# A decoder layer on one core: where the PSUM-freeing copies, the first left operand of the up projection and the block sums of the gates stand in the program

## The chip, the core and the metric

The kernel runs on one core of a Trainium2 chip. The metric is the device time of one execution in microseconds. The core has a matrix engine (PE, with its weight loads listed as PEld), a vector engine (DVE), a scalar engine (ACT), a general engine (POOL) and a sync engine (SP) that issues transfers. POOL issues transfers too, in this kernel most of the stores and the loads of large operands. Each engine works through its own list of instructions in the order in which the program gave them, and waits on semaphores where an instruction needs another engine's result.

## The reference

One pre-norm decoder layer on 1024 tokens plus 16 meta tokens, model width 1024, in float32. Cut to what matters here:

```
h = rms_norm(x, norm1_w)
(rq, rk, rv, rg, dq, dk, dv, cb, cc, cx, gates) = [h @ w_in[:, s:e] for s, e in column_bounds()]
ret  = retention(...) * silu(rg);  diff = diff_attention(...);  conv = cb * short_conv(cc * cx, conv_w)
g = sigmoid(gates).reshape(b, l, 3, 1024)
merged = g[:, :, 0] * (ret @ w_branch[0]) + g[:, :, 1] * (diff @ w_branch[1]) + g[:, :, 2] * (conv @ w_branch[2])
x = x + merged @ w_out
u = square(relu(rms_norm(x, norm2_w) @ w_up))       # 1024 -> 4096
y = rms_norm((x + u @ w_down)[meta tokens dropped], final_norm_w)
```

The inputs are float32 throughout, and so is the output of 1024 x 1024.

## The kernel before, in words

**Arithmetic.** Each float32 product is made of three matmuls on split operands (`split`, L134: ACT casts the high part, DVE subtracts it from the source for the low part): high times high, high times low, low times high. A matmul is 128 x 128 against 128 x 512.

**Stages.** First come the mixers and then the gates (24 column blocks, loop at L748), whose order a scheduler with a timeline of its own sets. The gates loop also builds, in `branch_sums` (L725), the right-hand operands of the branch projections and stores them to DRAM, and at the turn n = 14 loads the first four of them (`SET`, L764, issued by SP). From then on the order is written by hand, in the loop at L1218 under `tc.manual_schedule()`: what the loop calls first stands first in every engine's list. It walks over 170 steps: 42 for the three branch projections, 16 for the output projection, 56 for the up projection, 56 for the down projection. The branch, up and down projections use a scheme of seven products for a 2 x 2 block matrix product. The class `Quad` (L787) holds two such block products, the pairs p = 0 and 1. A step is one product i (0 to 6) of a quad for both pairs, that is two halves of 12 matmuls (6 in the last block of the down projection). The operands of the seven products are named B11, B21, T1, B22, T2, T3, T4 in this order; T1 to T4 are differences and sums of blocks.

**Banks.** PSUM has 8 banks. In a quad, one bank per pair (`ch`) accumulates the products 0, 4, 5, 6, and another (`pt`) product 1 and later 2 and 3. A product that goes on accumulating in a bank has to wait until what the bank held was read: product 3 waits for ACT's copy of product 2 (L849, `keep`), product 5 for ACT's copy after product 4 (also L849), product 6 for DVE's add after product 5. This add is the first line of `use`: L927 in the branches, L1122 in the up projection, and in the down projection L1174, which stands behind another add, L1173. In the opening of the up projection a new `pt` bank comes free only with the add after product 1 of the quad whose product 1 came before.

**Work beside the steps.** `prep` makes the left operands (weights) of the step two ahead: combinations of blocks on DVE (L816), then the cast on ACT and the subtraction on DVE (L135, L136). The ring `w` has 5 buffers for them, so a cast for step s + 2 needs the matmuls of an earlier half to be over. `evac` reads the finished banks. The table `work` holds further jobs by step, such as splits of right-hand operands (L136 with tile `op`) and `sums` (L1133), which builds the operands of the down projection out of the results of the up projection: four DVE operations, two casts, two subtractions for each pair. Their results lie in the ring `X` of 16 tiles and are stored to DRAM by POOL (L1108).

**The opening of the up projection** (from S0 + 10 on; E0 = step 58 is its first step). Its right-hand operands are the normalised results of the output projection: `normalise` (L1058), for T1 to T4 a difference (L1075, L1080), and the split into the tile `op`. Steps 58 to 63 do products 0 and 1 of the first three quads, and step 64 begins with product 2, which needs T1.

**Order in one turn s of the loop:** `evac` of step s-1 for pair 1; the left operands of step s+2, both pairs; the matmuls of pair 0, then of pair 1; the jobs of `work`; `evac` of step s for pair 0; loads.

```
            if 0 < s <= N:
                steps[s - 1][3](1)
            ...
            if 0 <= s + LP < N:
                steps[s + LP][1]()
            ...
            for fn in work.get(s, ()):
                fn()
            if 0 <= s < N:
                steps[s][3](0)
```

## Time and profile before

| what | value |
|---|---|
| time, median of 3 runs (lowest to highest) | 2417.67 us (2417.62 to 2418.17) |
| the profiled execution: its own time | 2421.53 us |
| the profiled execution: its span | 2419.7 us |
| mean granted TensorE clock over the span | 0.983 |
| PE busy | 2315.2 us, 96% |
| DVE busy | 1604.9 us, 66% |
| ACT busy | 1070.8 us, 44% |
| POOL busy | 483.4 us, 20% |

The rows quoted further down come from the profiled execution, whose span leaves out some 1.8 us of its own time; times of places in the program are counted from the span's start. The granted clock is 1.00 at 2.4 GHz and 0.50 at 1.2 GHz. Busy shares are means over stages with different limits, so the stages are read one by one.

### The profile page before, as it was taken

How to read it: one execution, taken by the hardware profiler on the slowest of the kernel's cores; microseconds unless marked ns; L12 is line 12 of the kernel's file. 1: busy time of each engine (PE TensorE's matmuls, PEld its weight loads, DVE VectorE, ACT ScalarE, POOL GpSimd, SP SyncE). 2: the span in 40 equal slices, each digit the busy share in tenths (PEclk: the TensorE clock that was granted, in tenths of full speed). 3: DMA queues.
4: the chain of work that ended last, by engine and by line, in shares of the span. 5: the costliest groups of instructions: out<-in, count | busy, mean ns of one | idle time of the engine just before them, and what ended most of it. 6: DMA issues, size and time to landing. Idle time of an engine off the chain costs nothing. (4 is left out here: it accounts for less than half of the span.)

```text
span 2419.7 us, 32940 instructions
## 1 busy us (share of the span) xinstructions
PE 2315.2 (96%) x11854; PEld 2001.1 (83%) x11854; DVE 1604.9 (66%) x3276; ACT 1070.8 (44%) x2079; POOL 483.4 (20%) x643
## 2 busy tenths in 40 slices
PE   7999999999999999999899999999688999999997
PEld 7999999999999999988688787778566777777776
DVE  6776776776765666576455458776656666777685
ACT  5554654644643333234233323344445555543344
POOL 2132233233122212213232010000003222100003
PEclk9999999999999999999999999999889999999998
DMA  3111111111111111119987385546135546655322
GB/s 137 36 52 46 44 52 45 45 53 44 40 58 36 53 53 44 53 57 370 410 322 281 129 329 217 201 133 203 61 104 195 179 161 252 253 195 199 123 87 70
DMA packets 124725, 328.13 MB, mean 136 GB/s; under 512 B 15376, under 2 KB 19600, under 8 KB 116496
## 3 DMA queue, kind: packets, MB, share of 16 engines
q1 hardware_dynamic: 84912, 159.27, 19.1%
q0 software_dynamic: 39648, 166.75, 17.8%
q8 instruction: 93, 1.52, 0.2%
q14 instruction: 72, 0.59, 0.1%
HBM read 219.52 MB, written 106.43 MB: 135 GB/s over the span
## 5 line engine op out<-in xcount | busy, mean ns | idle before, releaser
L161 PE MATMUL pmm<-H,whi 128*128 128x512 f32 (+3 forms) x1640 | 574.5, 352 | 17.6 <-ACT H L196 8.4
L162 PE MATMUL pmm<-H,whi 128*128 128x512 f32 (+3 forms) x1640 | 574.5, 351 | 2.0 <-DVE H L197 1.9
L163 PE MATMUL pmm<-H,wlo 128*128 128x512 f32 (+3 forms) x1640 | 573.1, 351 | 0.0
L840 PE MATMUL pb<-op,w 128*128 128x512 f32 x1176 | 472.7, 402 | 64.9 <-ACT t L849 24.9
L842 PE MATMUL pb<-op,w 128*128 128x512 f32 x1176 | 466.9, 397 | 0.0
L841 PE MATMUL pb<-op,w 128*128 128x512 f32 x1176 | 466.7, 397 | 0.0
L136 DVE TENSOR_TENSOR w<-raw,w 128x512 fp32r<-128x512 f32 (+1 forms) x400 | 263.8, 670 | 250.3 <-ACT w L135 246.8
L135 ACT CAST w<-raw 128x512 fp32r<-128x512 f32 (+1 forms) x400 | 237.2, 603 | 395.5 <-PE pb L842 195.1
L161 PEld LDWEIGHTS pmm<-H,whi 128*128 128x128 f32 x1640 | 309.5, 189 | 43.9 <-ACT H L196 8.4
L162 PEld LDWEIGHTS pmm<-H,whi 128*128 128x128 f32 x1640 | 310.3, 189 | 27.7 <-DVE H L197 2.8
L840 PEld LDWEIGHTS pb<-op,w 128*128 128x128 f32 x1176 | 224.5, 191 | 130.6 <-ACT t L849 32.3
L163 PEld LDWEIGHTS pmm<-H,wlo 128*128 128x128 f32 x1640 | 309.7, 189 | 24.4
L136 POOL TENSOR_TENSOR wlo<-raw,whi 128x512 fp32r<-128x512 f32 x142 | 192.8, 1359 | 594.0 <-ACT whi L135 539.6
L842 PEld LDWEIGHTS pb<-op,w 128*128 128x128 f32 x1176 | 224.3, 191 | 52.5 <-DVE w L136 0.9
L841 PEld LDWEIGHTS pb<-op,w 128*128 128x128 f32 x1176 | 224.8, 191 | 49.8 <-issue 0.2
L135 ACT CAST whi<-raw 128x512 fp32r<-128x512 f32 x192 | 118.6, 618 | 172.9 <-issue 82.6
L1108 POOL DMA_DIRECT2D d<-X x130 | 69.5, 540 | 284.4 <-ACT X L1124 163.5
L816 DVE TENSOR_TENSOR raw<-raw,raw 128x512 f32<-128x512 f32 (+1 forms) x176 | 111.5, 662 | 5.8 <-DMA raw<-w_branch 4.0
L378 ACT ACTIVATE B<-B,nb 128x144 f32<-128x144 f32 (+3 forms) x64 | 50.6, 791 | 99.4 <-DVE nb L377 99.1
L849 ACT COPY t<-pb 128x512 f32<-128x512 f32 x132 | 74.5, 581 | 39.1 <-PE pb L842 39.0
L754 ACT ACTIVATE t<-t 128x512 f32<-128x512 f32 x48 | 30.3, 632 | 132.1 <-DVE t L250 132.1
L880 POOL DMA_DIRECT2D op<-d x36 | 19.3, 540 | 289.9 <-PE pb L842 287.8
(290 smaller groups left out, 3817.2 us busy)
## 6 DMA issues: line engine op xcount, KB each, us to landing
op<-d POOLq DMA_DIRECT2D x55, 1024.0 KB, 8.5
raw<-w_in SPq DMA_DIRECT2D x192, 256.0 KB, 2.6
d<-X POOLq DMA_DIRECT2D x146, 256.0 KB, 4.1
d<-w POOLq DMA_DIRECT2D x60, 512.0 KB, 7.5
raw<-w_up SPq DMA_DIRECT2D x76, 256.0 KB, 4.4
raw<-w_down SPq DMA_DIRECT2D x56, 256.0 KB, 4.1
d<-t POOLq DMA_DIRECT2D x48, 256.0 KB, 5.2
raw<-d SPq DMA_DIRECT2D x48, 256.0 KB, 6.6
```

Of the source, the lines that this page charges most:

```text
L135: a.copy(out=hi, in_=src)
L136: (eng or v).tensor_tensor(out=lo, in0=src, in1=f32(hi), op=ALU.subtract)
L161: nc.tensor.matmul(pt, lhsT=hi[:, s], rhs=xh[:, c0:c0 + w], start=start, stop=False)
L162: nc.tensor.matmul(pt, lhsT=hi[:, s], rhs=xl[:, c0:c0 + w], start=False, stop=False)
L163: nc.tensor.matmul(pt, lhsT=lo[:, s], rhs=xh[:, c0:c0 + w], start=False, stop=stop)
L378: a.activation(out=pt, in_=pt, func=AF.Exp, scale=slope, bias=nb, accum_out=st[:, m:m + 1])
L816: comb = lambda d, x0, x1, o: v.tensor_tensor(out=d, in0=x0, in1=x1, op=o)
L840: nc.tensor.matmul(pt, lhsT=w[0][:, s], rhs=b[0][:, k], start=first, stop=False, skip_group_check=True)
L841: nc.tensor.matmul(pt, lhsT=w[0][:, s], rhs=b[1][:, k], start=False, stop=False, skip_group_check=True)
L842: nc.tensor.matmul(pt, lhsT=w[1][:, s], rhs=b[0][:, k], start=False, stop=k == nk - 1, skip_group_check=True)
L849: a.copy(out=t, in_=pt)
L1108: at(fetch, now[0] + 1, lambda: G.dma_start(out=dst, in_=src))
```

## The change

It has three parts.

1. The loop of the hand-ordered steps. A new entry `copy` of each step takes the readings that free a bank within the quad: ACT's copies after products 2 and 4, and the add after product 5. In turn s, the copy of step s-1 for pair 1 now comes first, then `evac` of step s-1 for both pairs; the left operands of step s+2 come behind the matmuls of step s, and the copy of step s for pair 0 stands between the cast of the first and that of the second left operand, ahead of the jobs of `work`. `evac` of pair 0 thus moves from the end of turn s to the start of turn s+1, and the job `sums` of pair 0, which is entered one turn after it, moves one turn later. In `down_use` the add that reads the bank comes before the add that does not. The results (0, 0) of the pairs 4 and 5 of the up projection stay in the tile `t` of their copy.
2. The opening of the up projection. The differences of all blocks come first and the splits behind them, not block by block in turn; and the operands T2, T3, T4 are spread over the turns E0+4 to E0+8, before E0+4 to E0+6.
3. The gates. The block sums take every second turn from n = 6 on, and the loads of `SET` are entered one operand at a time at n = 9, 11, 13, 15, before all at n = 14.

```
+    SET = {}
...
-        if n >= 2 and sums_todo and n != 14:
+        if n >= 2 and sums_todo and (n < 6 or n % 2 == 0):
             branch_sums(*sums_todo.pop(0))
-        if n == 14:
...
-            for name in ORDER[:4]:
-                SET[name] = [opnd(True, [P, 4, 512]) for _ in range(2)]
-                for z in range(2):
-                    nc.sync.dma_start(out=f32(SET[name][z]), in_=TD[2][name][:, z])
+        if 9 <= n < 17 and n % 2 == 1:
+
+            name = ORDER[(n - 9) // 2]
+            SET[name] = [opnd(True, [P, 4, 512]) for _ in range(2)]
+            for z in range(2):
+                nc.sync.dma_start(out=f32(SET[name][z]), in_=TD[2][name][:, z])
...
-        def prep(self, i):
+        def prep(self, i, half):
...
-            for p in range(2):
+            for p in range(2) if half == 0 else ():
...
-            for p in range(2):
-                self.op(i, p, r[p, (0, 1, 4, 1, 4, 0, 3)[i]])
+            self.op(i, half, r[half, (0, 1, 4, 1, 4, 0, 3)[i]])
...
+        def keep(self, pt):
+            t = temp("t", [P, 512])
+            a.copy(out=t, in_=pt)
+            return t
+
+        def copy(self, i, p):
+
+            if i == 5:
+                self.use(p, 1, 1, self.kept["ch", p], self.kept["p5", p])
+            elif i == 2:
+                self.kept["p5", p] = self.keep(self.kept["pt", p])
+            elif i == 4:
+                self.kept["u2", p] = self.keep(self.kept["ch", p])
...
-            elif i == 2:
-                K["p5", p] = keep(K["pt", p])
             elif i == 4:
-                self.use(p, 0, 1, K["pt", p], keep(K["ch", p]))
-            elif i == 5:
-                self.use(p, 1, 1, K["ch", p], K["p5", p])
+                self.use(p, 0, 1, K["pt", p], K["u2", p])
...
     def up_t1(ks):
         for k in ks:
             normalise(0, 1, k)
-            v.tensor_tensor(out=blk(0, 1, k), in0=blk(0, 1, k), in1=blk(0, 0, k), op=ALU.subtract)
-            up_op("T1", k, blk(0, 1, k))
-
-    def up_sum(name, dst, x0, x1):
-        for k in range(4):
-            v.tensor_tensor(out=blk(*dst, k), in0=blk(*x0, k), in1=blk(*x1, k), op=ALU.subtract)
-            up_op(name, k, blk(*dst, k))
+        differ((0, 1), (0, 1), (0, 0), ks)
+        up_ops("T1", (0, 1), ks)
...
-    at(work, E0 + 1, lambda: up_t1(range(2)))
-    at(work, E0 + 2, lambda: up_t1(range(2, 4)))
-    at(work, E0 + 3, lambda: plain_op("B22", range(4)))
-    at(work, E0 + 4, lambda: up_sum("T2", (1, 1), (1, 1), (0, 1)))
-    at(work, E0 + 5, lambda: up_sum("T3", (0, 0), (1, 1), (0, 0)))
-    at(work, E0 + 6, lambda: up_sum("T4", (1, 0), (1, 0), (1, 1)))
...
+    for n, fn in ((1, lambda: up_t1((0, 1))), (2, lambda: up_t1((2, 3))), (3, lambda: up_plain("B22", range(4))),
+                  (4, lambda: differ((1, 1), (1, 1), (0, 1))), (5, lambda: up_ops("T2", (1, 1), range(4))),
+                  (6, lambda: differ((0, 0), (1, 1), (0, 0))), (6, lambda: up_ops("T3", (0, 0), range(4))),
+                  (7, lambda: differ((1, 0), (1, 0), (1, 1))), (8, lambda: up_ops("T4", (1, 0), range(4)))):
+        at(work, E0 + n, fn)
...
-            u = U[r, j] = temp(FIRST_U[pair] if pair < 4 and (r, j) == (0, 0) else "X", [P, 512])
+            if pair in (4, 5) and (r, j) == (0, 0):
+                u = sb
+            else:
+                u = temp(FIRST_U[pair] if pair < 4 and (r, j) == (0, 0) else "X", [P, 512])
+            U[r, j] = u
...
-            v.tensor_tensor(out=sb, in0=sb, in1=xc, op=ALU.add)
-        v.tensor_tensor(out=xc, in0=pt, in1=xc if sb is None else sb, op=ALU.add)
+            v.tensor_tensor(out=sb, in0=pt, in1=sb, op=ALU.add)
+        v.tensor_tensor(out=xc, in0=pt if sb is None else sb, in1=xc, op=ALU.add)
...
             if 0 < s <= N:
+                steps[s - 1][4](1)
+                steps[s - 1][3](0)
                 steps[s - 1][3](1)
             for fn in soon.get(s, ()):
                 fn()
-            if 0 <= s + LP < N:
-                steps[s + LP][1]()
             if 0 <= s < N:
                 steps[s][2](0)
                 if s in mid:
                     mid[s]()
                 steps[s][2](1)
+            if 0 <= s + LP < N:
+                steps[s + LP][1](0)
+            if 0 <= s < N:
+                steps[s][4](0)
+            if 0 <= s + LP < N:
+                steps[s + LP][1](1)
             for fn in work.get(s, ()):
                 fn()
-            if 0 <= s < N:
-                steps[s][3](0)
```

**What moves on ACT in a branch step.** The first place is ACT's list about step 16, product 2 of the third branch quad, where the right-hand operands of the next branch are split too. `COPY t` frees a bank, `CAST w` makes a left operand, `CAST op` is half of a split of a right-hand operand. Before:

```order
L135 CAST op_14866<-op_14867 128x512
L135 CAST op_14913<-op_14914 128x512 x2
L849 COPY t_15004<-pb_14972 128x512
L849 COPY t_15010<-pb_14985 128x512
L135 CAST w_15014<-raw_14760 128x512
L135 CAST w_15017<-raw_14762 128x512
L135 CAST op_14913<-op_14914 128x512 x2
```

Now:

```order
L845 COPY t_14995<-pb_14966 128x512
L135 CAST w_14997<-raw_14903 128x512
L135 CAST op_14864<-op_14865 128x512
L135 CAST op_14911<-op_14912 128x512 x2
L845 COPY t_15010<-pb_14979 128x512
L135 CAST w_15038<-raw_14757 128x512
L135 CAST w_15041<-raw_14759 128x512
```

The copy of pair 0 has moved ahead of the second cast of a left operand and of the three casts for the right-hand operands; the copy of pair 1 still stands behind them, and ahead of the next two casts.

**What moves on DVE in the opening.** The second place is DVE's list between the two left operands of product 3 and the adds that free the banks for product 2, step 64. L1080 and (now) L1075 are the differences; L136 with `op` is the second half of a split, which waits for ACT's cast of the same block; L1122 and (now) L1126 are the adds. Before:

```order
L136 TENSOR_TENSOR w_17138<-raw_17064,w_17138 128x512
L136 TENSOR_TENSOR w_17141<-raw_17066,w_17141 128x512
L1080 TENSOR_TENSOR X_16169<-X_16722,X_16169 128x512
L136 TENSOR_TENSOR op_17172<-X_16169,op_17171 128x512
L1080 TENSOR_TENSOR X_16215<-X_16771,X_16215 128x512
L136 TENSOR_TENSOR op_17172<-X_16215,op_17171 128x512
L1080 TENSOR_TENSOR X_16262<-X_16812,X_16262 128x512
L136 TENSOR_TENSOR op_17172<-X_16262,op_17171 128x512
L1080 TENSOR_TENSOR X_16305<-X_16853,X_16305 128x512
L136 TENSOR_TENSOR op_17172<-X_16305,op_17171 128x512
L1122 TENSOR_TENSOR X_17184<-pb_17144,t_17130 128x512
L1122 TENSOR_TENSOR X_17188<-pb_17157,t_17132 128x512
```

Now:

```order
L136 TENSOR_TENSOR w_17154<-raw_17060,w_17154 128x512
L136 TENSOR_TENSOR w_17157<-raw_17062,w_17157 128x512
L136 TENSOR_TENSOR op_17161<-X_16722,op_17160 128x512
L136 TENSOR_TENSOR op_17161<-X_16771,op_17160 128x512
L136 TENSOR_TENSOR op_17161<-X_16812,op_17160 128x512
L136 TENSOR_TENSOR op_17161<-X_16853,op_17160 128x512
L1126 TENSOR_TENSOR t_17120<-pb_17124,t_17120 128x512
L1126 TENSOR_TENSOR t_17122<-pb_17137,t_17122 128x512
L136 TENSOR_TENSOR w_17202<-raw_17106,w_17202 128x512
L136 TENSOR_TENSOR w_17207<-raw_17108,w_17207 128x512
L1075 TENSOR_TENSOR X_16169<-X_16722,X_16169 128x512
L1075 TENSOR_TENSOR X_16215<-X_16771,X_16215 128x512
```

T3's differences (X_16169 and on) and splits have moved behind the two adds; ahead of the adds stand the four subtractions of T2's split (`op_17161`), whose differences were issued a turn earlier, so that no difference stands between two of them.

**What moves on SP in the gates.** The third place is SP's list at the loads of `SET` (L764); L146 loads a weight tile of a gate block, L731 a block for `branch_sums`. Before:

```order
L146 DMA raw_12816<-w_in 128x512
L731 DMA raw_12783<-d_118 128x512
L146 DMA raw_12822<-w_in 128x512
L731 DMA raw_12785<-d_118 128x512
L764 DMA op_13516<-d_12025 128x2048
L764 DMA op_13517<-d_12025 128x2048
L764 DMA op_13520<-d_12026 128x2048
L764 DMA op_13521<-d_12026 128x2048
L146 DMA raw_12921<-w_in 128x512
```

Now:

```order
L146 DMA raw_12781<-w_in 128x512
L731 DMA raw_12853<-d_118 128x512
L146 DMA raw_12787<-w_in 128x512
L731 DMA raw_12855<-d_118 128x512
L764 DMA op_12956<-d_12025 128x2048
L764 DMA op_12957<-d_12025 128x2048
L764 DMA op_13135<-d_12026 128x2048
L764 DMA op_13136<-d_12026 128x2048
L146 DMA raw_12886<-w_in 128x512
```

Nothing has moved here but the numbers of the buffers. This holds for the lists of all five engines up to the end of the gates.

## Rows read from the trace of the kernel before

**Rows 1.** Waits of PE: line, releaser, total us, times, longest.

```profile
PE pb L840 <- ACT t L849: 24.9, 15, 6.3
PE pb L840 <- DVE X L1122: 22.8, 9, 16.3
PE pb L840 <- DVE X L1174: 8.3, 4, 3.1
PE pmm L161 <- ACT whi L135: 5.0, 1, 5.0
```

**Rows 2.** Busy us by stretch: length, PE, PEld, DVE, ACT, POOL, clock, DMA.

```profile
1697.60:1796.90 99.30, 70.76 (x269) 55.24 (x268) 61.08 (x94) 44.98 (x77) 1.62 (x3) 0.85 0.15 49
1796.90:1860.20 63.30, 56.05 (x241) 44.73 (x240) 40.64 (x64) 34.39 (x60) 19.16 (x36) 1.00 0.61 214
1860.20:2065.70 205.50, 197.43 (x841) 157.96 (x840) 128.72 (x203) 115.34 (x202) 55.12 (x103) 0.99 0.57 204
2065.70:2305.60 239.90, 234.17 (x1009) 188.38 (x1008) 173.44 (x274) 101.81 (x183) 16.60 (x31) 1.00 0.49 183
2305.60:2332.70 27.10, 22.64 (x85) 17.29 (x85) 23.41 (x47) 13.81 (x31) 1.07 (x2) 0.88 0.29 98
```

**Rows 3.** The same view, for stretches in which the granted clock was low.

```profile
1199.90:1206.70 6.80, 6.15 (x15) 4.80 (x16) 3.79 (x6) 3.83 (x7) 0.99 (x2) 0.50 1.04 403
1541.20:1548.00 6.80, 5.83 (x14) 4.57 (x15) 6.70 (x12) 1.58 (x4) 0.00 (x0) 0.50 0.48 157
1732.40:1739.20 6.80, 5.99 (x14) 4.82 (x15) 4.86 (x9) 4.06 (x7) 0.00 (x0) 0.50 0.01 2
1746.00:1763.10 17.10, 5.03 (x12) 3.99 (x13) 10.30 (x16) 6.63 (x11) 0.00 (x0) 0.50 0.12 35
1769.90:1776.70 6.80, 4.20 (x10) 3.32 (x11) 3.88 (x6) 2.30 (x5) 0.00 (x0) 0.50 0.31 98
```

**Rows 4.** PE's timeline: start, us, instruction, idle before it and its releaser.

```profile
1458.76 0.50 PE L840 MATMUL pb<-op,w 128*128 128x512 f32 x1 [3.42 <-ACT t L849]
1542.17 0.79 PE L840 MATMUL pb<-op,w 128*128 128x512 f32 x1 [3.46 <-ACT t L849]
1733.21 0.77 PE L840 MATMUL pb<-op,w 128*128 128x512 f32 x1 [5.70 <-DVE g L1122]
1758.07 0.76 PE L840 MATMUL pb<-op,w 128*128 128x512 f32 x1 [16.31 <-DVE X L1122]
1772.51 0.79 PE L840 MATMUL pb<-op,w 128*128 128x512 f32 x1 [6.31 <-ACT t L849]
2058.53 0.50 PE L840 MATMUL pb<-op,w 128*128 128x512 f32 x1 [2.51 <-DVE X L1122]
```

**Rows 5.** ACT's timeline ahead of the matmul at 1458.76.

```profile
1455.54 1.13 ACT L135 CAST w<-raw 128x512 fp32r<-128x512 f32 x2
1456.58 1.65 ACT L135 CAST op<-op 128x512 fp32r<-128x512 f32 x3
1458.14 1.05 ACT L849 COPY t<-pb 128x512 f32<-128x512 f32 x2
```

**Rows 6.** DVE's timeline in the opening of the up projection.

```profile
1732.38 0.68 DVE L1122 TENSOR_TENSOR g<-pb,t 128x512 f32<-128x512 f32 x1
...
1736.11 1.29 DVE L136 TENSOR_TENSOR w<-raw,w 128x512 fp32r<-128x512 f32 x2 [1.25 <-ACT w L135]
...
1750.70 0.69 DVE L136 TENSOR_TENSOR op<-X,op 128x512 fp32r<-128x512 f32 x1 [0.69 <-ACT op L135]
...
1757.24 1.28 DVE L1122 TENSOR_TENSOR X<-pb,t 128x512 f32<-128x512 f32 x2
```

**Rows 7.** The page's costliest groups: busy us, mean ns, idle before, releaser.

```profile
L135 ACT CAST w<-raw 128x512 fp32r<-128x512 f32 (+1 forms) x400 | 237.2, 603 | 395.5 <-PE pb L842 195.1
```

**Rows 8.** The page's transfers: issues, KB each, median us from issue to landing.

```profile
d<-X POOLq DMA_DIRECT2D x146, 256.0 KB, 4.1
```

**Rows 9.** The same of the stretch 2035 to 2064 us alone.

```profile
d<-X POOLq DMA_DIRECT2D x14, 256.0 KB, 11.8
```

More of the change, by code (lines that the diff above doesn't have):

```diff
@@ L842, in pe @@
                 nc.tensor.matmul(pt, lhsT=w[1][:, s], rhs=b[0][:, k], start=False, stop=k == nk - 1, skip_group_check=True)
+        def keep(self, pt):
[9 more added lines that the diff above has]
+                self.kept["u2", p] = self.keep(self.kept["ch", p])
         def evac(self, i, p):
             K = self.kept
-            def keep(pt):
-                t = temp("t", [P, 512])
-                a.copy(out=t, in_=pt)
-                return t
             if i == 0:
-                K["p1", p] = keep(K["ch", p])
+                K["p1", p] = self.keep(K["ch", p])
             elif i == 1:
                 self.use(p, 0, 0, K["pt", p], K["p1", p])
-            elif i == 2:
-                K["p5", p] = keep(K["pt", p])
             elif i == 4:
-                self.use(p, 0, 1, K["pt", p], keep(K["ch", p]))
-            elif i == 5:
-                self.use(p, 1, 1, K["ch", p], K["p5", p])
+                self.use(p, 0, 1, K["pt", p], K["u2", p])
             elif i == 6:
@@ L903, in product_step @@
     def product_step(q, i):
-        steps.append((lambda: q.load(i), lambda: q.prep(i), lambda p: q.pe(i, p), lambda p: q.evac(i, p)))
+        steps.append((lambda: q.load(i), lambda p: q.prep(i, p), lambda p: q.pe(i, p), lambda p: q.evac(i, p), lambda p: q.copy(i, p)))
     def pairs_of(w, quad):
@@ L997, in load_x, with prep @@
             nc.sync.dma_start(out=self.x, in_=x[:, self.f, META + self.j * 512:META + self.j * 512 + 512])
-        def prep(self):
-            for z in range(2):
-                w = temp("w", [P, 2, 512], F32R)
-                split(self.raw[z], w[:, 0], w[:, 1])
-                self.w.append(w)
+        def prep(self, z):
+            w = temp("w", [P, 2, 512], F32R)
+            split(self.raw[z], w[:, 0], w[:, 1])
+            self.w.append(w)
         def pe(self, p):
@@ L1039, in trunk_kernel @@
             at(fetch, s + 1, o.store)
-            steps.append((o.load, o.prep, o.pe, o.evac))
+            steps.append((o.load, o.prep, o.pe, o.evac, lambda p: None))
     def token_scale(j):
@@ L1058, in normalise, with up_ops, up_plain, differ @@
         v.scalar_tensor_tensor(out=xc, in0=xc, scalar=vec[:, V_N2 + f:V_N2 + f + 1], in1=R2[j], op0=ALU.mult, op1=ALU.mult)
-    def up_op(name, k, src):
-        if k == 0:
+    def up_ops(name, src, ks):
+        if name not in US:
             open_op(US, name, 4, name in U_LEFT)
-        split(src, US[name][0][:, k], US[name][1][:, k])
-    def plain_op(name, ks):
-        z, j = PLAIN[name]
         for k in ks:
-            normalise(z, j, k)
+            split(blk(*src, k), US[name][0][:, k], US[name][1][:, k])
+    def up_plain(name, ks):
         for k in ks:
-            up_op(name, k, blk(z, j, k))
+            normalise(*PLAIN[name], k)
+        up_ops(name, PLAIN[name], ks)
+    def differ(dst, x0, x1, ks=range(4)):
+        for k in ks:
+            v.tensor_tensor(out=blk(*dst, k), in0=blk(*x0, k), in1=blk(*x1, k), op=ALU.subtract)
     def up_t1(ks):
@@ L1086, in trunk_kernel @@
         for z in range(2):
-            at(work, S0 + 10 + 2 * n + z, lambda name=name, z=z: plain_op(name, (2 * z, 2 * z + 1)))
-    at(work, E0 + 1, lambda: up_t1(range(2)))
-    at(work, E0 + 2, lambda: up_t1(range(2, 4)))
-    at(work, E0 + 3, lambda: plain_op("B22", range(4)))
-    at(work, E0 + 4, lambda: up_sum("T2", (1, 1), (1, 1), (0, 1)))
-    at(work, E0 + 5, lambda: up_sum("T3", (0, 0), (1, 1), (0, 0)))
-    at(work, E0 + 6, lambda: up_sum("T4", (1, 0), (1, 0), (1, 1)))
+            at(work, S0 + 10 + 2 * n + z, lambda name=name, z=z: up_plain(name, (2 * z, 2 * z + 1)))
+    for n, fn in ((1, lambda: up_t1((0, 1))), (2, lambda: up_t1((2, 3))), (3, lambda: up_plain("B22", range(4))),
[3 more added lines that the diff above has]
+        at(work, E0 + n, fn)
     BLOCKS = ((0, 4), (4, 4), (8, 4), (12, 2))
```

1 line of the change is left out of this document (removed).

## The prediction

> **What bounds the kernel now.** PE is busy for 96% of the span, so the time is PE's work plus what PE waits for, plus what it loses at the low clock. I read PE's waits first. Those that belong to the hand-ordered steps have three releasers: ACT's copies (L849), 24.9 us in 15 waits; the adds of the up projection (L1122), 22.8 us; the adds of the down projection (L1174), 8.3 us [rows 1]. All three read a bank, and no wait of weight on a transfer stands among them. Next I read busy time by stage, to see where the waits lie: the opening of the up projection has 70.8 us of PE in 99.3, the rest of the first three up quads 56.1 in 63.3, the other five up quads 197.4 in 205.5, the first three blocks of the down projection 234.2 in 239.9, and the first quad of the last block 22.6 in 27.1 with DVE busy for 23.4 of them [rows 2]. From the fourth of these, a matmul costs 234.17 / 1009 = 0.232 us at full clock, a half step of twelve 2.8, a step 5.6. Then the clock: after the long waits it is granted at 0.50, and a matmul costs 5.83 / 14 = 0.42 [rows 3], so each one there loses 0.19. Last comes PE's timeline for the single waits and what ended them [rows 4].
>
> **Part one, the order of the loop.** It adds no instruction. It sets ACT's copies and the adds after product 5 ahead of work that is not due, and takes them stage by stage.
>
> *Branches.* At 1458.76 and 1542.17 PE stood 3.42 and 3.46 us for a copy [rows 4]. ACT was not idle then: ahead of the copies it cast two left operands and three blocks of a right-hand operand, 1.13 + 1.65 us [rows 5]. By the new order the copy of pair 0 is past the second cast and these three, but the copy of pair 1 still stands behind the casts for the right-hand operand. What is late next is that second copy and the left operand, so I leave about 1.45 of each wait and take 2.0 off each. With such short waits I take the low clock behind them as gone, as in the stretch from 1796.90, which has short waits alone and a clock of 1.00 [rows 2]: 14 x 0.19 = 2.6 for the later one [rows 3], and by estimate two thirds of that, 1.7, for the earlier. Two smaller waits of the same sort give about 1. Together 2.0 + 2.0 + 2.6 + 1.7 + 1 = 9.3; if the low clock stays, 5.
>
> *Up projection after the opening.* The idle time is 7.25 us in two quads and 8.07 in five [rows 2], and the mean clock of 0.99 in the five costs another 2, most of it likely behind the wait of 2.51 at 2058.53 [rows 4]. The copies and the adds come earlier here too, but `sums` of pair 0 has moved one turn on, next to the last of the other pair's adds and two combined left operands. I count twelve DVE operations in that turn, at 1.28 / 2 = 0.64 us each [rows 6] 7.7 us, in a step of 5.6. So product 3 of the next quad should stall by about 1.1 once a quad where it did not. Of the five quads I leave about 5 of the 10 us and gain 5 (bounds 2 and 7); in the other two 1.5 (bounds 0 and 2).
>
> *Down projection.* Product 6 waits for L1174, which stood behind L1173, an add with no bank in it [rows 1]. Now the add on the bank is first and has been issued before the left operands. In the first three blocks PE idles for 5.73 us [rows 2]; I take all but half a microsecond of that, and 0.8 for halves that these waits lengthen without showing as idle: 6.0 (bounds 4.5 and 7.5). In the first quad of the last block the steps are half as long with the same DVE work per step, so DVE is the bound: 23.4 us busy in 27.1 [rows 2]. With the adds in front DVE should work without a pause, and some of its work can slide to the next quad, so I take 22.8: 4.3 less (bounds 2 and 5). Its second quad and the tail I leave, with 2 either way, since PE's own order differs there.
>
> *Costs of this part.* Left operands are now made behind the matmuls of the step, ACT's copies wait for PE at the head of ACT's list, and the casts wait behind them. The cover is there: casts of left operands already waited for PE to finish a half and free a buffer, 195.1 us in all [rows 7], and that half is the one the copy waits for. So the cost is nothing as long as the cast and subtraction for step s + 2 end within step s + 1, 5.6 us against about 1.3. Without that cover, each of 154 steps would lose a cast and a subtraction, 1.3 us. The Trainium skill, page "TensorE: Matmul & The Clock Gate", section "Architectural detail: the array is 16× 32×32, not 1× 128×128", says that ACT and DVE take their queues strictly in order, which speaks against a waiting copy in front of casts; by that alone the change would cost something in every step. The trace agrees with the rule (the copies at 1458 stood behind casts), but also shows that the casts were waiting for the same half.
>
> **Part two, the opening.** Its waits are 5.70, 16.31 and 6.31 us [rows 4], together 28.3, and the low clock behind them costs (14 + 12 + 10) x 0.19 = 6.8 [rows 3]: 35 of the 36.9 us by which the stretch exceeds 269 x 0.232 [rows 2].
> The wait of 5.70 ends with an add that stands behind T1's and B22's splits. T1 went block by block, and DVE waited 0.69 us for ACT's cast in each [rows 6]. With all differences first these four waits go: 2.8, and 2.9 are left.
> The wait of 16.31 ends with the adds at 1757.24. From the adds at 1732.38 to these, DVE's list takes 24.9 us [rows 6]: T2's and T3's differences and splits, six combinations, four subtractions for left operands. By the new order the stretch holds twenty operations (two adds, six combinations, four subtractions for left operands, T2's four differences and four subtractions), 20 x 0.62 = 12.4, and one wait for casts of 1.3: 13.7, which is 11.2 less. The matmul at 1758.07 then starts at 1758.1 − 2.8 − 11.2 = 1744.1, and PE, which had run dry at 1741.8, does so at 1738.9 or, at full clock, somewhat sooner: a wait of 5 to 7.
> The wait of 6.31 ends with copies behind T4's casts; T4 is two turns later and the copy ahead of it: it goes. What is late next is the add after product 5 with T4's four subtractions before it, 2.5 us less some slack: 2.
> Left are 2.9 + 6 + 2, one stretch of low clock behind the 6 (2.5) and about 1.5 of little ones: 15. The gain is 35 − 15 = 20 (bounds 12 and 24).
>
> **Part three, the gates.** The lists of all engines are the same up to the end of the gates, so the pauses there stay, such as the 5.0 us for a cast whose data come late [rows 1] under a DMA share of 1.04 [rows 3]. I take 0.
>
> **Sum.** 9.3 + 20 + 1.5 + 5 + 6.0 + 4.3 = 46.1. All lower bounds together (branches 5, tail −2) give 23.5, all upper ones (branches 10, tail 2) 57.5. Against the profiled execution's own 2421.5 the sum makes 2375.4. The median of the runs lies 3.9 below that execution, so I predict 2371.5; the bounds all at once give 2394 and 2360.
>
> **Rivals.**
> *The stalls only move.* The opening stays DVE-bound, and if its waits come out like 5 and 9 instead of 2.9 and 6, each brings its stretch of low clock (2.6 + 2.2), and the up quads stall at product 3 as often as they gain. Then the opening gives 10, the up projection 2, the rest 19.6: 31.6, so 2386. For it: DVE is busy for 61 of the 99 us there [rows 2], more than any engine but PE, and the order of DVE is my count. Against it: the operations moved past the adds are in the listing.
> *More than I count.* No low clock is left in the opening, and product 3 does not stall: 8 more, 2363.5. The Trainium skill, page "TensorE: Matmul & The Clock Gate", section "HAM oscillation — how this bites in real kernels", tells that idle time of PE brings the low clock back. By it, shorter waits would win twice; here the waits of 3.42 to 16.31 us are followed by a clock of 0.50, which agrees.
> *The third part works.* If the gates' transfers did spread, the 5.0 and the slow matmuls behind it, 15 x 0.18 = 2.7 [rows 3], would go: 7.7 more, 2363.8. Against it stand the identical lists.
> *Slower than before.* The results of `sums` come one turn later, so their stores do, and the ring X of 16 tiles is written again later: an add of the next quad then waits for a store, and the bank behind it holds up PE. A store lands 4.1 us after its issue as a median [rows 8], and 11.8 in the crowded stretch before the down projection [rows 9]; my estimate from the order of the ring leaves some 3 us beyond the 4.1. The place is the adds L1126 in eight up quads, and the gain of 46 is lost where each quad waits about 6 us more, that is with stores landing after some 13 us throughout. With DMA busy for about 0.6 there I don't believe it: with 8 us each, 2435.
>
> **How the numbers follow.** The forecast, 2364 to 2380, has a chance of 0.66; stalls that only move (2381 to 2393) 0.18; more than counted (2355 to 2364) 0.06; the gates working 0.03; the change doing nothing that can be told 0.03; slower 0.04. The range of 8 in 10 runs from 2358 to 2390 and so takes in most of the second and third case. A measurement of this kernel tells about 0.2% (4.8 us) from no change. Faster 0.93, same 0.03, slower 0.04.
>
> **What would show it.** In the changed profile the waits on L849 should fall from 24.9 us to under 9, those on the down adds from 8.3 to under 2, and the list of low-clock stretches should lose those at 1459 and 1541 and two of the three in the opening. The opening should last about 79 us, the first quad of the last block under 24. The pauses of the gates stay word for word. I am wrong if the opening lasts over 87 us, if the waits on L1126 after the opening grow to over 10, or if casts of left operands, which PE hardly waits for now, turn up among PE's releasers.

## The result and the profile after

The changed kernel takes 2375.7 us (median of 4 runs, 2375.1 to 2376.4) against 2417.9 (2417.6 to 2418.3) of the kernel before on the same chip: a ratio of 0.9825, with a 95% interval of 0.9808 to 0.9842, 42 us less. The forecast was 2371.5, with a range of 2358 to 2390. The profiled execution took 2376.36 us, its span is 2374.6, 45.1 less than before.

The waits of PE in the changed kernel that bear on the terms (columns as in [rows 1]; L845 is the copy that was L849, L1126 the add that was L1122, L1177 the add of the down projection that reads the bank):

```profile
PE pb L839 <- DVE t L1126: 8.0, 1, 8.0
PE pb L839 <- ACT t L845: 7.9, 9, 1.4
PE pb L839 <- DVE X L1126: 7.7, 4, 2.5
PE pmm L161 <- ACT whi L135: 5.2, 1, 5.2
PE pb L839 <- DVE t L930: 3.4, 4, 1.2
PE pb L839 <- DVE t L1177: 2.6, 2, 2.1
```

Waits for copies have fallen from 24.9 us to 7.9, the longest from 6.3 to 1.4; the wait of 16.3 has become one of 8.0; the waits for the adds of the down projection have fallen from 8.3 to 2.6. The wait for a cast in the gates, 5.2, is still there.

The stages, from the view of busy time by stretch (columns as in [rows 2]; the branches, the opening, two up quads, five up quads, three blocks of the down projection, the first quad of its last block):

```profile
1359.20:1599.60 240.40, 234.28 (x1008) 188.19 (x1009) 178.29 (x276) 87.69 (x155) 15.51 (x29) 1.00 0.60 221
1688.50:1766.60 78.10, 66.33 (x269) 51.80 (x268) 58.03 (x93) 42.42 (x75) 1.62 (x3) 0.93 0.19 62
1766.60:1829.00 62.40, 57.36 (x242) 45.97 (x241) 40.14 (x64) 35.09 (x63) 19.17 (x36) 0.97 0.62 220
1829.00:2031.50 202.50, 195.78 (x842) 156.73 (x841) 129.36 (x204) 113.79 (x203) 54.49 (x102) 1.00 0.57 204
2031.50:2263.10 231.60, 231.60 (x1010) 189.08 (x1009) 174.35 (x276) 101.55 (x183) 17.23 (x33) 1.00 0.52 193
2263.10:2288.10 25.00, 22.16 (x86) 16.70 (x85) 23.44 (x47) 13.71 (x31) 1.07 (x2) 0.90 0.32 106
```

Set beside the same stretches before, of which the branches took

```profile
1360.10:1608.80 248.70, 238.63 (x1009) 191.65 (x1010) 180.26 (x277) 88.08 (x155) 15.51 (x29) 0.98 0.58 215
```

the terms of the sum come out as follows.

| place | forecast, us less | measured, us less |
|---|---|---|
| branches | 9.3 | 248.7 - 240.4 = 8.3 |
| opening of the up projection | 20 | 99.3 - 78.1 = 21.2 |
| two up quads | 1.5 | 63.3 - 62.4 = 0.9 |
| five up quads | 5 | 205.5 - 202.5 = 3.0 |
| three down blocks | 6.0 | 239.9 - 231.6 = 8.3 |
| first quad of the last block | 4.3 | 27.1 - 25.0 = 2.1 |
| all else (gates 0) | 0 | 45.1 - 43.8 = 1.3 |
| sum | 46.1 | 45.1 |

The single waits that answer to [rows 4], in PE's timeline after:

```profile
1454.80 0.50 PE L839 MATMUL pb<-op,w 128*128 128x512 f32 x1 [1.36 <-ACT t L845]
1535.12 0.50 PE L839 MATMUL pb<-op,w 128*128 128x512 f32 x1 [1.27 <-ACT t L845]
1720.79 0.47 PE L839 MATMUL pb<-op,w 128*128 128x512 f32 x1 [2.46 <-DVE g L1126]
1734.64 0.77 PE L839 MATMUL pb<-op,w 128*128 128x512 f32 x1 [8.04 <-DVE t L1126]
```

3.42 and 3.46 us have become 1.36 and 1.27, 5.70 has become 2.46, 16.31 has become 8.04, and 6.31 is gone. DVE's timeline between the adds of the opening (beside [rows 6]) shows why the fourth is as long as it is:

```profile
1720.55 0.68 DVE L1126 TENSOR_TENSOR k<-pb,t 128x512 f32<-128x512 f32 x1
1721.15 1.28 DVE L816 TENSOR_TENSOR raw<-raw,raw 128x512 f32<-128x512 f32 x2
1723.69 1.29 DVE L136 TENSOR_TENSOR w<-raw,w 128x512 fp32r<-128x512 f32 x2 [1.26 <-ACT w L135]
1724.90 2.49 DVE L1075 TENSOR_TENSOR X<-X,X 128x512 f32<-128x512 f32 x4
1727.31 2.74 DVE L816 TENSOR_TENSOR raw<-raw,raw 128x512 f32<-128x512 f32 x4
1729.97 1.51 DVE L136 TENSOR_TENSOR w<-raw,w 128x512 fp32r<-128x512 f32 x2
1731.40 2.49 DVE L136 TENSOR_TENSOR op<-X,op 128x512 fp32r<-128x512 f32 x4
1733.81 1.28 DVE L1126 TENSOR_TENSOR t<-pb,t 128x512 f32<-128x512 f32 x2
```

DVE works from 1720.55 to 1733.81 with one pause of 1.26, which is a left operand's; no subtraction of T2's split (`op`) waits for its cast any more. What is left of the wait is DVE's work ahead of the two adds: six combinations, four subtractions for left operands, T2's differences and splits.

### The profile page after: what moved, and what is told of

Its sections match the earlier page's. It is cut to its first block, busy times and chain, and to the rows that moved or that the text cites. A ratio compares the mean times of both kernels' runs of the same rounds, so it can differ in the third digit from the quotient of the medians.

```text
span 2374.6 us, 32955 instructions
## 1 busy us (share of the span) xinstructions
PE 2302.7 (97%) x11854; PEld 1994.7 (84%) x11854; DVE 1602.0 (67%) x3276; ACT 1066.7 (45%) x2079; POOL 484.8 (20%) x643
## 3 DMA queue, kind: packets, MB, share of 16 engines
q8 instruction: 93, 1.52, 0.3%
## 5 line engine op out<-in xcount | busy, mean ns | idle before, releaser
L136 DVE TENSOR_TENSOR w<-raw,w 128x512 fp32r<-128x512 f32 (+1 forms) x400 | 263.6, 670 | 229.2 <-ACT w L135 226.8
L162 PEld LDWEIGHTS pmm<-H,whi 128*128 128x128 f32 x1640 | 310.8, 190 | 26.8 <-DVE H L197 2.1
L136 POOL TENSOR_TENSOR wlo<-raw,whi 128x512 fp32r<-128x512 f32 x142 | 194.0, 1367 | 592.9 <-ACT whi L135 548.0
L839 PEld LDWEIGHTS pb<-op,w 128*128 128x128 f32 x1176 | 222.2, 189 | 95.3 <-ACT t L845 12.1
L841 PEld LDWEIGHTS pb<-op,w 128*128 128x128 f32 x1176 | 222.2, 189 | 51.5 <-DVE w L136 0.9
L840 PEld LDWEIGHTS pb<-op,w 128*128 128x128 f32 x1176 | 222.4, 189 | 49.1 <-issue 0.2
L845 ACT COPY t<-pb 128x512 f32<-128x512 f32 x132 | 76.3, 584 | 105.8 <-PE pb L841 105.5
L378 ACT ACTIVATE B<-B,nb 128x144 f32<-128x144 f32 (+3 forms) x64 | 50.6, 791 | 99.3 <-DVE nb L377 99.1
```

The lines of the kernel that those rows point to most:

```text
L136: (eng or v).tensor_tensor(out=lo, in0=src, in1=f32(hi), op=ALU.subtract)
L162: nc.tensor.matmul(pt, lhsT=hi[:, s], rhs=xl[:, c0:c0 + w], start=False, stop=False)
L378: a.activation(out=pt, in_=pt, func=AF.Exp, scale=slope, bias=nb, accum_out=st[:, m:m + 1])
L839: nc.tensor.matmul(pt, lhsT=w[0][:, s], rhs=b[0][:, k], start=first, stop=False, skip_group_check=True)
L840: nc.tensor.matmul(pt, lhsT=w[0][:, s], rhs=b[1][:, k], start=False, stop=False, skip_group_check=True)
L841: nc.tensor.matmul(pt, lhsT=w[1][:, s], rhs=b[0][:, k], start=False, stop=k == nk - 1, skip_group_check=True)
```

## The experiments

Each kernel was run on a chip beside the kernel before. The medians of the kernel before in the three sessions were 2419.8, 2420.0 and 2418.0 us, over 2414.4 to 2423.5. The changed kernel was run again in the last session alone, so most results stand beside its 2375.7 us across chips; differences of 2 or 3 us are read from the stages of the profiles, not from the times.

**The first part alone.** The kernel before with the new order of the loop, the copies and the order of the down adds, and nothing of the opening and the gates. The results of pairs 4 and 5, which the list of changes counts under this part, keep a tile of their own here:

```
+                steps[s - 1][4](1)
+                steps[s - 1][3](0)
                 steps[s - 1][3](1)
...
+            if 0 <= s + LP < N:
+                steps[s + LP][1](0)
+            if 0 <= s < N:
+                steps[s][4](0)
```

> The kernel before with the first part of the change alone (order of the loop, copies, order of the adds in the down projection; the results of pairs 4 and 5 keep their own tile). Theory: the gain adds up by place. Outside the opening it is what the changed kernel gained there, 45 - 21 = 24 us of span; in the opening the wait of 6.31 us for a copy goes with the slow matmuls behind it, about 8, while the waits of 5.70 and 16.31 stay. Sum 32, about 2386 us. Rival: the opening's three waits all hang on DVE's block-by-block splits, and the copy only comes as late by another way; then 24, about 2394 us.

Measured: 2393.0 us (2392.6 to 2393.2), 26.8 less than the kernel before: between theory and rival, and 1 us from the rival. Outside the opening the gain is as the theory has it, but the opening has shrunk by 3.4 us only:

```profile
1688.80:1784.70 95.90, 69.49 (x269) 54.31 (x268) 59.86 (x93) 43.32 (x75) 1.62 (x3) 0.86 0.16 51
```

and PE's timeline in it shows the wait for the first copy gone and another in its place:

```profile
1749.21 0.77 PE L839 MATMUL pb<-op,w 128*128 128x512 f32 x1 [16.67 <-DVE X L1124]
...
1763.77 0.79 PE L839 MATMUL pb<-op,w 128*128 128x512 f32 x1 [4.05 <-ACT t L845]
```

ACT's timeline ahead of the second shows why:

```profile
1762.62 0.62 ACT L135 CAST op<-X 128x512 fp32r<-128x512 f32 x1 [1.36 <-DVE X L1082]
1763.14 0.58 ACT L845 COPY t<-pb 128x512 f32<-128x512 f32 x1
```

The copy of pair 1 still stands behind T4's block-by-block casts, as the rival had it: of the 8 us that the theory gave to the first part here, it brings under half.

**The second part alone.** The kernel before with the new opening and pairs 4 and 5 in the tile of their copy (the tile was not tried by itself). What moves here belongs to right-hand operands (T1 to T4), not to a left operand as the title says:

```
+    for n, fn in ((1, lambda: up_t1((0, 1))), (2, lambda: up_t1((2, 3))), (3, lambda: up_plain("B22", range(4))),
...
+            if pair in (4, 5) and (r, j) == (0, 0):
+                u = sb
```

> The kernel before with the second part alone (opening by due turns, differences first, pairs 4 and 5 in the tile of their copy). Theory: the waits of 5.70 and 16.31 us shrink by about 3 and 8 to 11, and the wait for a copy stays in part, since that copy still stands behind the jobs of its turn: a gain of 12 to 17, 2401 to 2406 us. Rival: the second part alone brings the whole 21 us of the opening: about 2397 us.

Measured: 2401.7 us (2401.2 to 2404.0), 18.1 less than the kernel before in that session: in time inside the theory's range, in gain just above its 17. The opening takes 81.4 us, 17.9 less than the 99.3 of before. The two parts bring 17.9 and 3.4 there, together the 21.2 of the changed kernel, and 18.1 + 26.8 = 44.9 in all, where the whole change brings 42.2 in one session and 42.9 in another. So they add up, but for 2 to 3 us, which is no more than the medians of the kernel before differ between sessions.

**The third part alone.** The kernel before with the new entries in the gates:

```
-        if n >= 2 and sums_todo and n != 14:
+        if n >= 2 and sums_todo and (n < 6 or n % 2 == 0):
             branch_sums(*sums_todo.pop(0))
```

> The kernel before with the third part alone (block sums and loads of the first operands entered at other turns of the gates). Theory: the scheduler puts every instruction where it stood, so the time is that of before, 2417.7 us within 1. Rival: the part works by something that the order of the instructions does not show, such as other buffers: 2 us or more less than before.

Measured: 2419.5 us (10 runs) beside 2419.8, a ratio of 1.0003 (0.9993 to 1.0012). The third part does nothing that can be told from zero.

**The third part made to work.** The changed kernel, with the block sums and the loads of `SET` tied behind the weight loads of their turn on SP's list:

```
+            with tc.issue_after(getattr(last_w[0], "ins", last_w[0])):
+                branch_sums(*sums_todo.pop(0))
...
+            with tc.issue_after(getattr(last_w[0], "ins", last_w[0])):
+                for z in range(2):
+                    nc.sync.dma_start(out=f32(SET[name][z]), in_=TD[2][name][:, z])
```

> The changed kernel, in which the loads of the block sums and of the first operands are tied on SP's list behind the weight loads of the turn where they are entered, so that they really are spread. Theory: the two pauses of the gates (5.2 and 2.5 us) come from weight tiles queued behind a burst of transfers; they shrink or go, with the slow matmuls behind them: 7 to 12 us less than the changed kernel, 2364 to 2369 us. Rival: the stage moves data for 0.84 of its time anyway, so that the pause only turns up elsewhere: within 3 us of 2375.7.

Measured: 2372.7 us (2370.0 to 2374.4), some 3 less than the changed kernel: less than the theory said, and by the time alone at the edge of the rival's 3. The stage tells them apart. The two pauses for a cast are gone, and so is the low clock behind them (1.00 over the gates, where the changed kernel has 0.98). PE's waits in the gates are then

```profile
PE pmm L164 <- DVE wlo L136: 3.0, 3, 1.2
PE ps L164 <- DVE wlo L136: 1.1, 2, 0.6
PE pb L842 <- DVE t L251: 0.8, 1, 0.8
PE pmm L162 <- ACT whi L135: 0.7, 1, 0.7
```

and the stage takes 269.9 us in place of 274.2. About 4 us of new, short waits for DVE have taken the place of the 7.7, so the rival is right in part.

**The two adds of the down projection in their old order**, all else as changed:

```
-            v.tensor_tensor(out=sb, in0=pt, in1=sb, op=ALU.add)
-        v.tensor_tensor(out=xc, in0=pt if sb is None else sb, in1=xc, op=ALU.add)
+            v.tensor_tensor(out=sb, in0=sb, in1=xc, op=ALU.add)
+        v.tensor_tensor(out=xc, in0=pt, in1=xc if sb is None else sb, op=ALU.add)
```

> The changed kernel with the two adds of the down projection in their old order (the one that reads the bank comes second). Theory: the down projection gained 8 us in its first three blocks because the add now stands ahead of left operands and of the jobs of its turn, and the order of the two adds is worth at most its own 0.6 us per quad: 0 to 3 us more than the changed kernel, 2376 to 2379 us, with the 42 steps at 232 to 235 us. Rival: the order of the adds is what frees the bank in time; then the 42 steps go back to about 240 us and the time to about 2384.

Measured: 2377.4 us (2376.3 to 2378.6), and 232.4 us for the 42 steps in place of 231.6. The theory holds: the order of the two adds is worth 0.8 us there. By elimination it is the place of the add in the turn that counts, and the next run shows it.

**The readings of pair 0 behind the jobs of its turn** (the entry `copy`, that is both copies and the add after product 5), all else as changed:

```
-            if 0 <= s < N:
-                steps[s][4](0)
             if 0 <= s + LP < N:
                 steps[s + LP][1](1)
             for fn in work.get(s, ()):
                 fn()
+            if 0 <= s < N:
+                steps[s][4](0)
```

> The changed kernel with the copy (or add) of pair 0 behind the jobs of its turn and the second left operand; all else as changed. Theory: what the first part of the change gains in the branches is this place: the waits of 3.4 us come back in two quads with slow matmuls behind them, and in the opening the copy stands behind the splits again: 8 to 12 us more, 2384 to 2388. Rival: what counts is the copy of pair 1 and the later left operands, and pair 0 has slack: within 3 us of 2375.7.

Measured: 2407.1 us (2406.5 to 2408.0), 31 more than the changed kernel, far beyond the theory's 8 to 12. The waits of 3.4 us in the branches are back as it said, and branches and output projection together take 8.0 us more. The 42 steps of the down projection take 236.4, 4.8 more. But half of the loss lies in the five up quads, which take 218.1 us in place of 202.5: the readings now also stand behind `sums`, which has kept its new turn, and every one of the five waits at product 3. In the kernel before, with the readings as late but `sums` a turn earlier, the five took 205.5. So the 31 us belong to the two places together. Two of those waits show the clock's part in it:

```profile
1858.68 0.50 PE L839 MATMUL pb<-op,w 128*128 128x512 f32 x1 [2.44 <-ACT t L845]
1901.95 0.50 PE L839 MATMUL pb<-op,w 128*128 128x512 f32 x1 [2.43 <-ACT t L845]
```

and the view of busy time by stretch around them:

```profile
1857.10:1863.90 6.80, 5.22 (x16) 4.17 (x17) 6.41 (x11) 3.21 (x7) 3.76 (x8) 0.75 0.88 285
1900.30:1907.10 6.80, 5.15 (x23) 4.26 (x24) 6.68 (x12) 3.33 (x7) 2.66 (x5) 1.00 0.88 283
```

The same wait, in quads of the same instructions: behind the one the clock falls and 16 matmuls run in 6.8 us, behind the other it stays and 23 do.

**The left operands ahead of the matmuls again**, copies and results where the change put them:

```
+            if 0 <= s + LP < N:
+                steps[s + LP][1](0)
+                steps[s + LP][1](1)
             if 0 <= s < N:
                 steps[s][2](0)
```

> The changed kernel with the left operands of step s + 2 ahead of the matmuls of step s again, as before the change; copies and results stay ahead of the jobs of the turn. Theory: making the left operands later neither costs nor gains, since their casts wait for a half of matmuls in either place; the copy of pair 0 now stands behind both casts, which wait for the same half: 0 to 4 us more, 2376 to 2380. Rival 1: the later left operands are part of the gain, 10 us or more above 2375.7. Rival 2: a copy that waits ahead of casts costs something in every step, and this order wins it back: under 2374.

Measured: 2381.4 us (2380.1 to 2383.2) beside 2375.1 for the changed kernel on the same chip (its second run, below). That is 6 more, under rival 1's 10; rival 2 falls. About 2 us of the difference lie ahead of the branches, which this edit doesn't touch, and the other 4 are the theory's upper end. Waits for copies grow from 8.8 us in that second run to 11.8, since the copy of pair 0 comes a cast later: product 3 of the five up quads waits 1.40 us in place of 0.88, and the five take 205.2 us instead of 202.4.

**The job `sums` of pair 0 one turn earlier**, where it stood before the change:

```
-                at(work, now[0] + 1 + p, sums)
+                at(work, now[0] + 2 * p, sums)
```

> The changed kernel with the block sums of pair 0 in the up projection one turn earlier, where they stood before the change. Theory: the wait of 0.88 us ahead of product 3 in five quads comes from these sums, six DVE operations ahead of the adds after product 1, so it goes: five times 1.2 us less, the 35 steps at 196 to 198 us in place of 202.5, about 2370 us. Rival: the turn that they move to is as full, and the wait only changes its place: 202 us, 2375 to 2376.

Measured: 2371.0 us (2368.6 to 2371.3), 4.7 less than the changed kernel. The five up quads take

```profile
1830.20:2026.00 195.80, 194.10 (x842) 157.20 (x841) 129.24 (x204) 114.27 (x203) 53.47 (x100) 1.00 0.59 207
```

6.7 us less than in the changed kernel, and no quad of theirs waits at product 3. So moving `sums` by a turn cost the change these 6.7 us, with the copies in their new place.

**The add after product 5 of pair 0 ahead of both left operands** (`early` holds the steps of product 5):

```
+            if s in early:
+                steps[s][4](0)
             if 0 <= s + LP < N:
                 steps[s + LP][1](0)
-            if 0 <= s < N:
+            if 0 <= s < N and s not in early:
                 steps[s][4](0)
```

> The changed kernel with the add after product 5 of pair 0 ahead of both left operands (the copies after products 2 and 4 stay between them). Theory: the waits ahead of product 6 (2.45 us in two up quads, 1.1 in the first, 0.7 in two branch quads, 1.2 and 0.8 in one) end with an add that stands behind a subtraction, which waits for a cast behind a chain of activations; with the add in front they go for the most part: 6 to 9 us less, 2367 to 2370. Rival: the left operands, now behind the add and so behind the matmuls of pair 0, come late, and PE waits for them instead: 2375 or more.

Measured: 2368.6 us (2367.9 to 2369.1), 7.1 less than the changed kernel and inside the theory's range. The two up quads take 58.4 us in place of 62.4 and the end of the opening 1.4 less; a wait of 1.52 for the other pair's add is what is left of 2.45. The rival's late left operands are not among PE's waits.

**All three improvements together.**

> The changed kernel with three of the edits tried one at a time: the gates' transfers tied to their turns, the block sums of pair 0 one turn earlier, the add after product 5 of pair 0 ahead of the left operands. Theory: their gains lie in different places and add up: 3 to 4 in the gates, 6.7 in five up quads, 7 in the waits ahead of product 6: 2375.7 - 17 = 2358 to 2361 us. Rival: the sums and the add use the same free time of DVE, so that one of them loses its gain: 2363 to 2366.

Measured: 2360.2 us (2359.4 to 2362.9, 5 runs), a ratio of 0.9765 to the kernel before (0.9752 to 0.9779), and 14.9 less than the changed kernel on the same chip. The five up quads take 194.2 us and the two 58.5: the gains add up, inside the theory's range. This is the fastest version found.

**The changed kernel once more.**

> The changed kernel once more, beside the two others on one chip, so that differences under 1% can be read: 2375.7 us within 1.5, with every stage as in its first profile within half a microsecond but for what the granted clock does behind waits of 1 to 2.5 us.

Measured: 2375.1 us (2373.7 to 2377.3). All stretches agree with the first profile within half a microsecond, except the first quad of the last block of the down projection (24.1 in place of 25.0). There PE waits once, for 2.07 us, where in the first profile it waits twice, for 2.10 and 0.51, and the mean clock is 0.93 in place of 0.90.

## Why the prediction came out right

**What bounds it.** Right: waits for readings of banks, released by copies and adds. The first part's new places for them, above all that of pair 0's readings ahead of the jobs, carry the gain outside the opening, as the run with those readings behind the jobs shows. In the opening it is the second part, by the runs of either part alone.

**Branches, 9.3, measured 8.3.** The remaining waits were taken at about 1.45 and are 1.36 and 1.27, without low clock: PE's busy time fell by 238.6 - 234.3 = 4.3, the 2.6 + 1.7 of the sum. But product 6 of two of these quads, which did not wait before, now waits 0.7 in each for an add behind the left operand, and a third waits 2.0 where it waited 1.8 (together the 3.4 us for L930). The sum did not have this; the run with that add in front takes the 3.4 down to 2.4.

**Opening, 20, measured 21.2.** The wait of 5.70 was taken down to 2.9 and is 2.46. DVE's stretch between the adds was taken at 13.7 and is 13.9 (1733.81 - 1719.95, the start of the first of the two adds). The wait came out at 8.04, not 5 to 7, because PE ran its matmuls ahead of it at full clock and was dry sooner; what the longer wait takes, those matmuls had won. The run with the add after product 5 in front bears this out: there PE ran them in part at low clock and waited 6.49, and step 64 began 46.2 us after the start of the opening in both. The add after product 5 was taken at 2 and costs 1.13.

**Up projection, 1.5 and 5, measured 0.9 and 3.0.** Here the mechanism was wrong in two places, and that the totals came near was partly luck. First, the prediction had product 3 "stall by about 1.1 once a quad where it did not". It did: before the change, each of the five quads waited 0.93 or 0.94 us there, and now each waits 0.88.

```profile
1878.13 0.50 PE L840 MATMUL pb<-op,w 128*128 128x512 f32 x1 [0.93 <-ACT t L849]
1846.81 0.50 PE L839 MATMUL pb<-op,w 128*128 128x512 f32 x1 [0.88 <-ACT t L845]
```

(The first line is of the kernel before, the second of the changed one.) The new place of the copy would have taken the old wait away, and the new turn of `sums` put another in its place:

| readings of pair 0 | `sums` of pair 0 | wait at product 3, us | run |
|---|---|---|---|
| behind the jobs | old turn | 0.93 | before |
| behind the jobs | a turn later | 2.44 (4.46 in the last quad) | readings behind the jobs |
| ahead of the jobs | a turn later | 0.88 | after |
| ahead of the jobs | old turn | none | `sums` one turn earlier |

(The first row is of the kernel before, whose left operands and readings of pair 1 stand elsewhere too; the other three differ in these two places alone.) The move of `sums` costs 6.7 us, where the sum left 5 for all waits of the five quads. Of the 3.0 gained there, 2.2 are the execution's: the kernel with the third part alone, whose instructions are those of before, took 203.3 us for these quads and not 205.5, with a wait of 2.03 at the place of the 2.51 and no low clock behind it. Nor is it DVE's surplus of work, twelve operations in a step, as the prediction counted: DVE's timeline in that turn has a pause of 2.46, behind the adds that stand after `sums`.

```profile
1842.56 1.28 DVE L1126 TENSOR_TENSOR X<-pb,t 128x512 f32<-128x512 f32 x2
1846.30 0.69 DVE L136 TENSOR_TENSOR w<-raw,w 128x512 fp32r<-128x512 f32 x1 [2.46 <-ACT w L135]
```

It is the order. ACT's timeline ahead of the wait in the changed kernel reads

```profile
1843.28 0.63 ACT L1127 ACTIVATE X<-X 128x512 f32<-128x512 f32 x1 [4.05 <-DVE X L1126]
1843.94 0.63 ACT L1128 ACTIVATE X<-X 128x512 f32<-128x512 f32 x1
1844.48 0.62 ACT L1127 ACTIVATE X<-X 128x512 f32<-128x512 f32 x1
1845.13 0.63 ACT L1128 ACTIVATE X<-X 128x512 f32<-128x512 f32 x1
1845.67 0.60 ACT L135 CAST w<-raw 128x512 fp32r<-128x512 f32 x1
1846.17 0.58 ACT L845 COPY t<-pb 128x512 f32<-128x512 f32 x1
```

ACT waits 4.05 us for adds that stand behind the sums on DVE, and only then gets through four activations and a cast to the copy. The Trainium skill, page "TensorE: Matmul & The Clock Gate", section "Architectural detail: the array is 16× 32×32, not 1× 128×128", has ACT and DVE take their queues strictly in order; these rows agree, and it is here, not at the copies that wait for PE, that the order is paid for.

Second, "The copies and the adds come earlier here too" does not hold for one add. In the two up quads the waits of 2.18 for a copy after product 4 are gone, but the add after product 5 of pair 0 still stands behind a left operand, and the wait for it has grown from 1.46 and 1.44 to 2.45 in each quad, in the first of them with low clock behind it (0.64 over 4.8 us):

```profile
1822.98 0.50 PE L840 MATMUL pb<-op,w 128*128 128x512 f32 x1 [1.46 <-DVE X L1122]
1791.19 0.50 PE L839 MATMUL pb<-op,w 128*128 128x512 f32 x1 [2.45 <-DVE X L1126]
```

(The first line is of the kernel before, the second of the changed one.) With that add in front, the two quads take 4 us less.

**Down projection, 6.0 and 4.3, measured 8.3 and 2.1.** In the three blocks PE has no idle time left (231.6 busy of 231.6), and 8.3 is beyond the upper bound of 7.5. PE's busy time there fell as well, from 234.2 to 231.6: matmuls stretched by short waits, for which the sum had 0.8 us in place of 2.6. That term was sized too small. In the last block DVE's busy time is the same 23.4 as before, as the prediction had it, but PE still waits 2.1 for an add and the clock falls behind it, so 25.0 (24.1 in the second run) and not 22.8.

**Cost of later left operands, 0.** They don't turn up among PE's releasers, and putting them back in front wins nothing. What their place costs is the wait for the add after product 5 above.

**Gates, 0.** Right, by the run of that part alone. The rival "the third part works" was priced at 7.7; made to work it brings 3.

**The step that was off: the median.** The terms sum to 46.1 against 45.1 measured, but the prediction also took off 3.9 us, the distance of the profiled execution of before from the median of three runs, as if the changed kernel had the same. It has 0.7 (2376.36 against 2375.7), and this makes most of the 4.2 us by which the result lies above the forecast. The 3.9 is no constant: in the three sessions the kernel before spread over 2414.4 to 2423.5, the changed one over 2373.7 to 2377.3. One source of such scatter is shown; that it made this 3.9 is not. The kernel with the third part alone has the same down projection as the kernel before; there the 42 steps took 242.7 us and not 239.9. It has one more wait for a copy, of 1.18, and behind a wait of 1.85 like that of 2220.40 before, matmuls ran at low clock (PE's timeline, and busy time by stretch as in [rows 2], where the clock stands third from the end):

```profile
2217.48 0.50 PE L840 MATMUL pb<-op,w 128*128 128x512 f32 x1 [1.85 <-DVE X L1174]
2218.50:2222.00 3.50, 3.50 (x11) 2.73 (x10) 0.92 (x2) 0.00 (x0) 0.00 (x0) 0.56 0.49 206
```

In the kernel before, the clock stayed:

```profile
2220.40 0.50 PE L840 MATMUL pb<-op,w 128*128 128x512 f32 x1 [1.85 <-DVE X L1174]
2219.00:2222.50 3.50, 2.10 (x9) 1.76 (x10) 3.20 (x6) 0.20 (x1) 0.38 (x1) 1.00 0.67 234
```

So one stage differs by 2 to 3 us between executions of the same instructions. That the six terms agree with their forecasts within 2.3 us says no more than that, and that their sum is off by 1.0 only is partly luck: three came out too small in the forecast, by 1.2, 2.3 and 1.3 us, and four too large, by 1.0, 0.6, 2.0 and 2.2.

**Rivals.** "The stalls only move" holds for the up quads and the last block, not for the opening. The later stores held nothing up: no add waits for one, and the slower side had no part in it. Of the signs named, two failed by little: the waits for the down adds are 2.6 and not under 2, the first quad of the last block 25.0 and not under 24.

## What to carry to other kernels

Where a bank is shared by successive products, look for what stands ahead of its reading on the list of the engine that reads it, and put that reading ahead of work that is not due; here the late place of one pair's readings cost 31 us, half of it where `sums` stood ahead of them. A job moved by the same edit has to be followed to the turn where it lands: six operations a turn later cost 6.7 us of the gain until they were moved back. Where a scheduler sets the order, entering code elsewhere may move nothing, which the listing of the built program tells before any run.

## What the runs showed of the hardware

Equal waits of PE were followed by either clock. A wait of 1.85 us had a mean clock of 0.56 over 3.5 us behind it in one execution and 1.00 in another; one of 2.44 was followed by low clock (0.75 over 6.8 us) and one of 2.43 in the same run by 1.00; in the changed kernel, of two waits of 2.45, the one at 1791.19 was followed by 0.64 over 4.8 us and the one at 1822.93 by 1.00. What decides it is not shown. The forecast had taken short waits as free of it, by one stretch where none was hit. The times of the kernel before spread over 9 us in 33 runs, those of the changed one over 4 in 8; that fewer such waits made the spread smaller is not shown, since fewer runs spread less too.
